# A ring of two halves of three groups, moved in 50688 bytes a partition, in place of six slots of one group

## The chip, the cores and the metric

The kernel runs on one core of a Trainium2 chip; the other cores have nothing to do with it. The metric is the device time of one execution in microseconds, less being better. Three engines of the core have work: VectorE (DVE) computes, SyncE (SP) issues every load, ScalarE (ACT) issues every store. The transfers themselves run on the core's 16 DMA engines.

## What is computed

The input has 8 batches of 4096 rows of 2112 float32 numbers. Every four rows that follow one another make a group; the mean of the group is taken from each of its rows.

```python
B, S, D = 8, 4096, 2112
stride = 4
x_r = x.reshape(B, S // stride, stride, D)
pooled = x_r.mean(axis=2)
upsampled = np.repeat(pooled, stride, axis=1)
return (x - upsampled).astype(np.float32)
```

So each number is read from HBM once and written once: 8 x 4096 x 2112 x 4 bytes = 276.8 MB in each direction. There is no reuse that could lessen it.

## The kernel before

Lines 27 to 37 look at the input as 8192 groups of 8448 numbers (four rows of 2112, which lie next to each other in HBM, 33792 bytes). One **tile** is 128 groups, one on each partition, 4224 KB in all; there are n = 64 tiles. A tile is a single run of 4.3 MB in HBM, and a load of it gives each partition a run of 33792 bytes.

Six slots in SBUF (line 46) hold one tile each; `pad` (line 45) only fills space ahead of them. Tile k goes through slot k mod 6, in place: loaded, changed by VectorE, stored from the same bytes. Two places for the sum take turns, `s_sb` in SBUF and `s_ps` in PSUM (lines 47 and 48).

The order of the work is written out by hand with semaphores inside `tile_critical` (line 78); no planner moves anything:

- **Loads** (lines 79 to 84) stand in the queue of SP, 64 in order. The load of tile k waits until the store of tile k-6 has landed, since both use one slot. The first six wait for nothing.
- **VectorE** (lines 86 to 90) runs `reduce_tile` for each tile, in a loop of 10 laps of six tiles, and four more behind it. Line 58 waits for the load. Line 59 adds rows 0 and 1 into the sum, line 62 adds rows 2 and 3 to it (two instructions of 2112 numbers a partition), and line 67 does x = sum * (-1/4) + x on all four rows at once, with the sum repeated by a stride of zero (one instruction of 8448 numbers). It then raises `done_sem`.
- **Stores** (lines 92 to 96) stand in the queue of ACT, 64 in order; the store of tile k waits for `done_sem` to reach k+1.
- SP waits at the end for the last six stores (lines 98 and 99).

Of the kernel before, what the change touches and what calls it, by code (L numbers as in the profile page):

```python
# [1 line left out]

# [4 lines left out]

STRIDE = 4
SLOTS = 6  # L10
PAD = 224


@with_exitstack
def kernel(
    ctx: ExitStack,
    tc: tile.TileContext,
    x: bass.AP,
    out: bass.AP,
):  # L20

    nc = tc.nc
    B, S, D = x.shape
    P = nc.NUM_PARTITIONS
    W = STRIDE * D  # L30
    G = (B * S) // STRIDE
    assert S % STRIDE == 0 and G % P == 0
    n = G // P

    xg = x.rearrange("b (g f) d -> (b g) (f d)", f=STRIDE)
    og = out.rearrange("b (g f) d -> (b g) (f d)", f=STRIDE)
    f32 = mybir.dt.float32

    pad_pool = ctx.enter_context(tc.tile_pool(name="pad", bufs=1))
    io_pool = ctx.enter_context(tc.tile_pool(name="io", bufs=1))  # L40
    sum_pool = ctx.enter_context(tc.tile_pool(name="sum", bufs=1))
    psum_pool = ctx.enter_context(
        tc.tile_pool(name="psum", bufs=1, space=bass.MemoryType.PSUM)
    )
    pad_pool.tile([P, PAD], f32, name="pad")
    slots = [io_pool.tile([P, W], f32, name=f"slot{b}") for b in range(SLOTS)]
    s_sb = sum_pool.tile([P, D], f32, name="s_sb")
    s_ps = psum_pool.tile([P, D], f32, name="s_ps")

    load_sems = [tc.alloc_semaphore(f"load{b}") for b in range(SLOTS)]  # L50
    store_sems = [tc.alloc_semaphore(f"store{b}") for b in range(SLOTS)]
    step_sem = tc.alloc_semaphore("step")
    done_sem = tc.alloc_semaphore("done")

    def reduce_tile(b, parity):
        rows = slots[b].rearrange("p (f d) -> p f d", f=STRIDE)
        s = s_ps if parity else s_sb
        nc.vector.wait_ge(load_sems[b], 16).then_inc(load_sems[b], -16)  # L58
        add = nc.vector.tensor_add(out=s[:], in0=rows[:, 0, :], in1=rows[:, 1, :])  # L59
        add.then_inc(step_sem)  # L60
        for f in range(2, STRIDE):
            add = nc.vector.tensor_add(out=s[:], in0=s[:], in1=rows[:, f, :])  # L62
            add._wait_ge(step_sem, f - 1)
            add.then_inc(step_sem)
        adds = STRIDE - 1
        nc.vector.wait_ge(step_sem, adds).then_inc(step_sem, -adds)  # L66
        nc.vector.scalar_tensor_tensor(  # L67
            out=rows,
            in0=s[:, None, :].to_broadcast([P, STRIDE, D]),
            scalar=-1.0 / STRIDE,  # L70
            in1=rows,
            op0=mybir.AluOpType.mult,
            op1=mybir.AluOpType.add,
        ).then_inc(done_sem)

    assert SLOTS % 2 == 0
    laps, rest = divmod(n, SLOTS)
    with tc.tile_critical():
        for k in range(n):
            b, lap = k % SLOTS, k // SLOTS  # L80
            load = nc.sync.dma_start(out=slots[b][:], in_=xg[k * P:(k + 1) * P])
            if lap:
                load._wait_ge(store_sems[b], 16 * lap)
            load.then_inc(load_sems[b], 16)

        with nc.vector.Fori(0, laps):
            for b in range(SLOTS):
                reduce_tile(b, b % 2)
        for b in range(rest):
            reduce_tile(b, b % 2)  # L90

        for k in range(n):
            b = k % SLOTS
            store = nc.scalar.dma_start(out=og[k * P:(k + 1) * P], in_=slots[b][:])
            store._wait_ge(done_sem, k + 1)
            store.then_inc(store_sems[b], 16)

        for k in range(n - SLOTS, n):
            nc.sync.wait_ge(store_sems[k % SLOTS], 16 * (k // SLOTS + 1))


# [1 line left out]
_INS = ['x']  # L103
_OUTS = [((8, 4096, 2112), 'float32')]


# [23 lines left out]
```

## Time and profile before

| What | Value |
|---|---|
| median of 10 executions | 1285.81 us (1285.6 to 1286.02) |
| the profiled execution, its own time | 1286.08 us |
| its span in the profile | 1284.3 us |
| moved by DMA | 553.66 MB, mean 431 GB/s |
| VectorE busy | 1026.5 us, 80% of the span |
| one load, issue to landing | least 12.6, median 59.7, most 91.2 us |
| one store, issue to landing | least 13.7, median 43.6, most 43.7 us |
| first load issued, first add | 0.95 us, 13.69 us |
| first store issued | 29.98 us |
| last load issued | 1192.89 us |
| last subtraction | starts at 1260.07 us, takes 8.96 us |

The span is the time between the first and the last thing in the profile of that one execution. The execution's own time is 1.8 us longer than the span, and 0.27 us over the median. In the profile a row of instructions gives the line, the engine, the operation, the tiles written and read, how many there were, their busy time in us and the mean of one in ns, and then the idle time of the engine ahead of them. In the views by stretches of time, the columns are the stretch, its length, the busy time of VectorE and GpSimd with the number of instructions, the granted clock of TensorE, the busy share of the 16 DMA engines, and the GB/s they moved.

### The profile page before, as it was taken

The page shows a single profiled execution, that of the slowest core. Times are in us where ns is not written, and L with a number is a line of the kernel's source. Part 1 is how long each engine was busy: PE and PEld are TensorE (multiplying, and loading weights), DVE is VectorE, ACT ScalarE, POOL GpSimd, SP SyncE. Part 2 cuts the span into 40 slices and gives each one's busy share as a digit, 9 for nine tenths or more (in the row PEclk, how much of TensorE's full clock was granted, in tenths as well). Part 3 has the DMA queues.
Part 4 walks back from the last instruction along what each step waited for, and adds up shares of the span by engine and source line. Part 5 has one row for each costly group of instructions (what it writes and reads, how often), then busy time and mean ns, then how long its engine had stood idle before and what let it go on. Part 6 is the DMA issues. An engine that isn't in the chain of part 4 may idle for free. (4 is left out here: it accounts for less than half of the span.)

```text
span 1284.3 us, 588 instructions
## 1 busy us (share of the span) xinstructions
DVE 1026.5 (80%) x256; POOL 0.2 (0%) x4
## 2 busy tenths in 40 slices
DVE  5998788787787877878778787787887878878775
POOL 0000000000000000000000000000000000000000
DMA  9999999999999999999999999999999999999999
GB/s 404 420 436 426 436 436 436 425 438 436 432 429 437 436 429 433 437 436 425 437 436 434 427 437 436 430 432 437 436 427 435 436 437 424 438 436 433 428 437 389
DMA packets 18433, 553.66 MB, mean 431 GB/s; under 512 B 2048, under 2 KB 2048, under 8 KB 2048
## 3 DMA queue, kind: packets, MB, share of 16 engines
q1 hardware_dynamic: 9216, 276.83, 50.0%
q10 hardware_dynamic: 9216, 276.83, 49.9%
q14 instruction: 1, 0.01, 0.0%
HBM read 276.82 MB, written 276.82 MB: 431 GB/s over the span
## 5 line engine op out<-in xcount | busy, mean ns | idle before, releaser
L67 DVE SCALAR_TENSOR_TENSOR slot<-s_sb,slot 128x8448 f32<-128x8448 f32 x32 | 286.7, 8958 | 4.7 <-DVEq L66 0.2
L67 DVE SCALAR_TENSOR_TENSOR slot<-s_ps,slot 128x8448 f32<-128x8448 f32 x32 | 286.6, 8957 | 4.7
L59 DVE TENSOR_TENSOR s_sb<-slot 128x2112 f32<-128x2112 f32 x32 | 75.4, 2357 | 120.7 <-DVEq L58 120.7
L59 DVE TENSOR_TENSOR s_ps<-slot 128x2112 f32<-128x2112 f32 x32 | 75.7, 2367 | 108.1 <-DVEq L58 108.1
L62 DVE TENSOR_TENSOR s_ps<-s_ps,slot 128x2112 f32<-128x2112 f32 x64 | 151.4, 2366 | 2.2
L62 DVE TENSOR_TENSOR s_sb<-s_sb,slot 128x2112 f32<-128x2112 f32 x64 | 150.9, 2358 | 2.2
L114 POOL MEMSET const-uint8-127<- 128x1 uint8 x1 | 0.1, 102 | 0.0
L114 POOL MEMSET const-bfloat16-1.0<- 128x1 bf16 x1 | 0.1, 101 | 0.0
L114 POOL MEMSET const-float32-0.0<- 128x1 f32 x1 | 0.1, 98 | 0.2 <-issue 0.2
L114 POOL MEMSET const-float32-1.0<- 128x1 f32 x1 | 0.1, 98 | 0.0
## 6 DMA issues: line engine op xcount, KB each, us to landing
slot<-in_x_dram SPq DMA_DIRECT2D x64, 4224.0 KB, 59.7
out_dram<-slot ACTq DMA_DIRECT2D x64, 4224.0 KB, 43.6
```

Source lines behind the costliest of these rows:

```text
L59: add = nc.vector.tensor_add(out=s[:], in0=rows[:, 0, :], in1=rows[:, 1, :])
L62: add = nc.vector.tensor_add(out=s[:], in0=s[:], in1=rows[:, f, :])
L67: nc.vector.scalar_tensor_tensor(out=rows, in0=s[:, None, :].to_broadcast([P, STRIDE, D]), scalar=-1.0 / STRIDE, in1=rows, op0=mybir.AluOp ...
L114: nc = _bacc.Bacc("TRN2", target_bir_lowering=False, num_devices=1)
```

## The change

The 64 tiles become 21 supers of three tiles each and one tile left over (21 x 3 + 1). A super is 384 groups; partition p now holds three groups that lie next to each other in HBM, 3p, 3p+1 and 3p+2 of the super (`adjacent`), a run of 101376 bytes. In place of six slots there is one ring of the same 6 x 33792 bytes a partition, in two halves of three groups.

A super is moved in two **parts** of one and a half groups, 50688 bytes a partition. So the first part holds the first group and the first two rows of the middle one, the second part the rest. In HBM the 128 runs of one transfer are 50688 bytes long and begin 101376 bytes apart; the other part fills the gaps. There are four parts in the ring, each with a semaphore for its load and one for its store. SP issues 42 loads of a part and one of the tile left over; ACT issues 42 stores of a part and two for the left over tile, of two rows each. The load of part i waits for the store of part i-4.

VectorE's loop runs 10 laps of two supers, and one super and the left over tile follow. In a super the first and last group are done as before. The middle group's first add is done ahead of the wait for the second part, the two others behind it, and its subtraction is two instructions of 4224 numbers a partition in place of one of 8448. The store of a super's first part waits for the first of these two (the second subtraction of the super), the store of its second part for the last subtraction of the super (the fourth).

```diff
-SLOTS = 6
+HALVES = 2
+SUPER = 3
+PARTS = 2
...
+    def adjacent(rows, k):
+
+        return rows.rearrange("(p j) w -> p (j w)", j=k)
...
-    slots = [io_pool.tile([P, W], f32, name=f"slot{b}") for b in range(SLOTS)]
+    ring = io_pool.tile([P, HALVES * SUPER * W], f32, name="ring")
...
+    n_parts = HALVES * PARTS
+    step = SUPER * W // PARTS
+    half_group = STRIDE // 2
...
+    for j in range(n_super):
+        src = adjacent(xg[j * SUPER * P:(j + 1) * SUPER * P], SUPER)
+        dst = adjacent(og[j * SUPER * P:(j + 1) * SUPER * P], SUPER)
+        for h in range(PARTS):
+            part = slice(h * step, (h + 1) * step)
+            a = (j % HALVES) * SUPER * W + h * step
+            moves.append((a, src[:, part], dst[:, part], subs * j + (2, subs)[h]))
...
+    def reduce_super(half, parity):
+        groups = [
+            Group((half * SUPER + j) * W, (parity + j) % 2) for j in range(SUPER)
+        ]
+        begin(half * PARTS)
+        groups[0].add(0, STRIDE)
+        groups[0].sub(0, STRIDE)
+        groups[1].add(0, half_group)
+        begin(half * PARTS + 1)
+        groups[1].add(half_group, STRIDE)
+        groups[1].sub(0, half_group)
+        groups[1].sub(half_group, STRIDE)
+        groups[2].add(0, STRIDE)
+        groups[2].sub(0, STRIDE)
+
+    def load(i, cols, src):
+        dma = nc.sync.dma_start(out=ring[:, cols], in_=src)
+        if i >= n_parts:
+            dma._wait_ge(store_sems[i % n_parts], 16 * (i // n_parts))
+        dma.then_inc(load_sems[i % n_parts], 16)
+
+    def store(i, cols, dst, done):
+        dma = nc.scalar.dma_start(out=dst, in_=ring[:, cols])
+        dma._wait_ge(done_sem, done)
+        dma.then_inc(store_sems[i % n_parts], 16)
...
+        with nc.vector.Fori(0, laps):
+            for half in range(HALVES):
+                reduce_super(half, half * SUPER % 2)
+        reduce_super(0, 0)
+        begin(len(moves) % n_parts)
+        last = Group(last_col, SUPER % 2)
+        last.add(0, STRIDE)
+        last.sub(0, half_group)
+        last.sub(half_group, STRIDE)
+
+        for i, (a, _, dst, done) in enumerate(moves):
+            store(i, slice(a, a + step), dst, done)
+        for h in range(2):
+            a = h * half_group * D
+            b = a + half_group * D
+            store(
+                len(moves),
+                slice(last_col + a, last_col + b),
+                og[last_rows, a:b],
+                subs * n_super + 1 + h,
+            )
```

`begin` is the wait for a part's load, `Group.add` the adds of a range of a group's rows and `Group.sub` the subtraction on a range of them, with the same instructions as before.

## The prediction, made before the changed kernel was run

> **What bounds the kernel now.** I read the page first. VectorE is busy 1026.5 of 1284.3 us, so it is not the bound. The row by slices and the queue rows say what is:
>
> ```profile
> DMA  9999999999999999999999999999999999999999
> ...
> q1 hardware_dynamic: 9216, 276.83, 50.0%
> q10 hardware_dynamic: 9216, 276.83, 49.9%
> ```
>
> The 16 DMA engines are busy in every slice, and the two queues together fill 99.9% of the span. Of 9216 packets in a queue, 8192 are runs of 33792 bytes (64 tiles x 128 partitions); the other 1024 are the ones under 512 B. Next the waits, to see whether VectorE or the transfers come last:
>
> ```profile
> DVE s_sb L59 <- DVEq L58: 120.7, 30, 13.7
> DVE s_ps L59 <- DVEq L58: 108.1, 30, 3.7
> ```
>
> VectorE waits some 3.7 us for the load of nearly each tile. The period is read from the timeline: the first add of tile 7 starts at 134.72, that of tile 63 at 1252.75, so (1252.75 - 134.72)/56 = 19.965 us a tile, in which 2 x 4224 KB (8.651 MB) pass: 433.3 GB/s. The view by stretches agrees, and shows loads alone (14 to 30), both (the next three) and stores alone (last):
>
> ```profile
> 14.00:30.00 16.00, 15.78 (x5) 0.00 (x0) 1.00 0.98 425
> 60.00:90.00 30.00, 29.57 (x9) 0.00 (x0) 1.00 1.01 436
> 90.00:120.00 30.00, 25.86 (x8) 0.00 (x0) 1.00 1.00 433
> 100.00:1100.00 1000.00, 803.96 (x201) 0.00 (x0) 1.00 1.00 433
> 1256.00:1280.00 24.00, 12.84 (x3) 0.00 (x0) 1.00 1.00 430
> ```
>
> The stretch 1281 to 1283 moves only 17 GB/s: the bytes end at about 1281. So the span is 2.3 us until the engines run, 64 x 19.965 = 1277.8 us of bytes, 3 us after the last byte, and about 1 us of ramp. Only three things can change the time: the rate, an interval without transfers, or the two ends. I take them in turn.
>
> **1. Intervals without transfers: 0.** This is where the ring could hurt, so I lay the new order out by hand with the old durations. A tile costs VectorE 16.17 us (13.69 to 29.86). A part is 6.488 MB: 15 us with the engines to itself, 30 us while loads and stores share them. Let the first part (A) of a super land at 0; the others then land at 30 (B), 60 and 90. First group: until 16.2. First add of the middle one: 18.6. Now the added wait: VectorE stands until B lands at 30, and queued behind that wait are the rest of this super and, through it, the store of A. Two adds (2 x 2.37) and half a subtraction (8.96/2) later, at 39.4, the store of A is issued; the other half ends at 43.9, the third group and with it the store of B at 60.0. VectorE is then done just as the next super's first part lands, so it keeps up: 48.7 us of work in 60. The subtraction cut in two adds at most one instruction's fixed part. By the rows 8958 ns for 8448 numbers is 1.060 ns each, so the 2358 ns add of 2112 holds about 118 ns beyond that: 0.12 us x 22 is 2.6 us, and the 228.8 us of waits above hide it. Uncovered, it would cost those 2.6 us.
>
> Does a part come back in time? A place is used every 4 x 30 = 119.8 us. For A: 30 loading, 39.4 held, 30 storing, so 20.4 us are left for standing in queues and for hand-overs (store landed, next load issued and running). For B: 30 + 30 + 30, so 29.8 left. One hand-over is at most 2.6 us by the first load (12.6 us to landing, 9.98 of them bytes). Two of them take 5.2 of the 20.4 us. So about 15 us of queue stand ready, less than now (119.8 - 16.2 - 2 x 20 = 63.6), but above zero. And as long as either queue holds a transfer, the engines are full: stores alone run at 430 above. Before the first store there is no hole either: it moves from 29.98 to about 45.5 us (A lands at 17.6, B at 32.6, then the steps above), but the four loads issued at the start hold the same 26 MB and last beyond 60 us. At the end the left over tile lands at 50 on the same clock; stores still queued then end at about 53, 68 (A), 83 (B), and 88 and 93 (the two halves), and VectorE has released these by 39, 60, 72 and 76. Each is ahead of its turn, so the engines run through to the last byte. What is late next after VectorE's waits is still the transfers.
>
> **2. The two ends: +0.3 us.** The first load is issued as early as now, the last byte is followed by the same 3 us. Only the stretch of loads alone grows, by 45.5 - 30 = 15.5 us. At 425 in place of 433 GB/s that costs 15.5 x 8/433 = 0.3 us; if the 425 is only the ramp, nothing.
>
> **3. The rate: between 0 and -2.6 us, -1.3 taken.** The runs grow from 33792 to 50688 bytes. There are 16384 of them now, and then 2 x 42 x 128 + 128 (the left over load) + 256 (its two stores) = 11136: 32% fewer. Transfers fall from 128 to 87. What a run costs beyond its bytes is not shown, as all have one size. From below: nothing, the rate belongs to the bytes; the 433 that stands in all long stretches speaks for that. From above: the best stretch of 30 us has 436; if the whole way from 433.3 to 436 (0.6% of 1277.8 = 7.9 us) were a fixed part of each run, 32% of it would go: -2.6 us. Both ends are as near to the rows (436 is one stretch whose edges blur by a packet or two), so I take the middle, -1.3. A loss of rate by the new pattern (runs 101376 bytes apart) has no row that shows it; it is bounded by 430 and 425, and priced as a rival.
>
> Here two rules of the Trainium skill can be set against the rows. "DMA: Bandwidth & Descriptors", section "Bandwidth", fits a transfer as 2.0 us and its bytes at 436 GB/s; 41 fewer transfers would then save 82 us. But by that fit the 128 transfers would take 1526 us in a row, and they take 1284.3: the fixed part lies under the next transfer here. The same page, "Where 436 GB/s comes from", sets a ceiling of 435.2 GB/s for the 16 engines; by it only 0.44%, 5.6 us by estimate, is left to win by any change of size, and 32% of that is 1.8 us. The same page's table of other facts tells of a rate halved where rows lie a large power of two apart, which speaks against spreading the runs; 101376 is not such a distance and no run here shows it.
>
> **Sum.** 0 + 0.3 - 1.3 = -1.0 us. The profiled execution took 1286.08 (span 1284.3 and 1.8 around it), so the changed one would take 1285.1 when profiled; that execution lies 0.27 over the median, so the median would be **1284.8 us**, -0.08%. A measurement of this kernel can tell about 0.2% (2.6 us) from no change.
>
> **The rivals.**
> - **Faster: the fixed parts are larger than I take them.** The share of 1.00 in the stretches is rounded, so up to 0.5% of 1277.8 us (6.4 us) could be gaps at the 128 hand-overs from transfer to transfer; 41 fewer save 2.0 us. With the full 2.6 us of the runs: -4.6, so 1281.2 us. For it: it takes only small fixed parts. Against it: the two queues overlap, so a gap in one is filled by the other. 0.15.
> - **Slower: the spread pattern lowers the rate.** Place: each load at line 131 and store at line 137. Today one transfer is one run of 4.3 MB; then it is 128 pieces, half of a 13 MB stretch. Price: at 430 GB/s (stores alone) 1277.8 x 3.3/430 = +9.8, so 1295.6; at 425, +25, so 1311. It decides from 432.4 GB/s down, which is +2.6. For it: rates of 425 to 436 show that direction or mixture may matter a little, and nothing in this trace was so spread. Against it: each piece is still 50 KB long. 0.14.
> - **Slower: the ring runs out.** If the 15 us of queue are used up (B's wait, hand-overs longer than 2.6 us), load and store queues are both empty once in each lap of 120 us. A hand-over each time, 2.6 us x 10, gives +26, so 1311 us. It decides once VectorE's hold and hand-overs together grow by those 15 us. 0.07.
> - **It does nothing measurable by itself.** Bytes set the time and the old fixed parts were hidden: 1285.8 to 1286.1. This lies in the bound of my forecast, as the forecast's small gain does.
>
> **How the numbers follow.** Forecast, 1283.2 to 1286.1, 0.62 (0.36 for a small gain, 0.26 for none); 0.02 for small losses within 0.2%; faster rival 0.15; slower rivals 0.14 and 0.07. That makes faster 0.15, same 0.64, slower 0.21. For 8 in 10 the range runs from the faster rival's 1281 to the 1295.6 of 430 GB/s; it leaves out the deeper half of the slower cases (0.11) and the gains above 4.8 us (0.05). The likeliest case's own range is 1283.2 to 1286.1.
>
> **What would show it.** Right: DMA still 9 in all 40 slices, 433 to 434 GB/s in the stretch 100 to 1100, first store issued near 45 us, VectorE waiting about 11 us at the wait for a second part and almost nothing at the one for a first part, loads landing after some 33 to 50 us rather than 59.7, and bytes ending 3 us ahead of the span's end. Step 1 is wrong if a slice falls under 9 or a long stretch under a DMA share of 0.99; step 3 if the share stays at 1.00 and the GB/s move away from 433 by over 1; step 2 if the first 60 us or the last 30 lose more than a microsecond against now.

## The result and the profile after

The changed kernel takes 1296.17 us (median of 8 executions, 1295.71 to 1297.12) against 1285.75 us: 1.0081 times as long, interval 1.0072 to 1.009. That is 10.4 us slower, where I had forecast 1.0 us less and a range that ended at 1295.6. The profiled execution took 1295.94 us (span 1294.2), 9.9 us over that of before. The median hides how far executions lie apart: of twelve on record, ten took 1295.7 to 1297.9 us, one 1289.6 and one 1285.8. Those of the kernel before stay within 0.5 us.

First the same two parts of the page as before, the slices and the queues:

```profile
DMA  9999999999999999999999999999999999999977
GB/s 401 426 442 436 426 434 442 426 428 447 429 426 443 434 426 440 437 426 436 439 428 432 437 432 426 440 431 431 439 429 434 439 429 429 439 434 426 435 340 339
...
q1 hardware_dynamic: 6192, 276.83, 49.6%
q10 hardware_dynamic: 6336, 276.83, 49.4%
```

There are a third fewer packets, as worked out. The engines are full through 38 slices, and the loss seems to be all in the last two (340 and 339 GB/s, where before had 437 and 389, as its own row shows):

```profile
GB/s 404 420 436 426 436 436 436 425 438 436 432 429 437 436 429 433 437 436 425 437 436 434 427 437 436 430 432 437 436 427 435 436 437 424 438 436 433 428 437 389
```

The view by stretches puts numbers to it (stretch, its length, busy time of VectorE and GpSimd, clock, DMA share, GB/s):

```profile
14.00:30.00 16.00, 10.87 (x4) 0.00 (x0) 1.00 1.00 434
100.00:1100.00 1000.00, 802.00 (x217) 0.00 (x0) 1.00 1.00 433
1250.00:1260.00 10.00, 9.82 (x3) 0.00 (x0) 1.00 0.59 256
1260.00:1270.00 10.00, 9.79 (x5) 0.00 (x0) 1.00 0.78 335
1280.00:1290.00 10.00, 0.00 (x0) 0.00 (x0) 1.00 0.77 329
```

From here one would say: the drain has an interval without transfers, since the store queue ran dry while VectorE still worked. The timeline of VectorE speaks against that as the whole story. These are the two adds that wait for the second part, early and late, and the last subtractions:

```profile
203.06 4.75 DVE L95 TENSOR_TENSOR s_sb<-s_sb,ring 128x2112 f32<-128x2112 f32 x2 [11.33 <-DVEq L83]
...
1231.87 4.77 DVE L95 TENSOR_TENSOR s_ps<-s_ps,ring 128x2112 f32<-128x2112 f32 x2 [11.27 <-DVEq L83]
...
1269.18 9.02 DVE L106 SCALAR_TENSOR_TENSOR ring<-s_ps,ring 128x4224 f32<-128x4224 f32 x2
```

The wait of 11 us for the second part is the one I had laid out. But (1231.87 - 203.06)/17 = 60.52 us a super, where 3 x 19.965 = 59.90 us went before, from these two rows, 56 tiles apart:

```profile
134.72 2.37 DVE L59 TENSOR_TENSOR s_ps<-slot 128x2112 f32<-128x2112 f32 x1 [3.73 <-DVEq L58]
...
1252.75 2.37 DVE L59 TENSOR_TENSOR s_ps<-slot 128x2112 f32<-128x2112 f32 x1 [3.74 <-DVEq L58]
```

The loads land later and later, by 0.6 us a super, though the sum of all engines still reads 433 GB/s.

What the sum hides is in the trace's records of single DMA packets (start, duration, bytes, queue). They don't name the engine; I followed each engine from a packet's end to the next packet's start, which gives 16 chains, without gaps until the end. Two chains that meet in phase can be taken for each other from there on, and in this trace two do, at 917 us. Durations of a run of 33792 bytes are 1251 ns before, nearly without exception; a run of 50688 takes 1872 ns. "Slow" is a packet of over 50 ns more, between 100 and 1230 us:

```
                slow loads  slow stores  excess, all  ends of the 16 engines: first, middle, last
before                   0            0       0.0 us  1281.4  1281.5  1282.3
after                   84            3      20.1 us  1287.9  1287.9  1292.5
```

After, load packets are at times 0.05 to 1.35 us late, and most of it falls on one chain: 6.86 us up to 917 us and 5.67 us behind it, 12.5 us in all. It is one engine on both sides of 917 us: its packets never pause and it ends at 1292.5, while each of the other 15 pauses for 6.7 to 8.4 us near the end. Its packets between 110 and 1200 us take 60.50 us a super, the period of the landings; without the lateness they would take 59.81. The kernel's semaphores ask for all 16 engines, so VectorE, the stores and the next loads go at the pace of the slowest. The pauses of the other 15, which end at 1242 and 1262 us, are what the stretches show. The sum is -1.8 us (rate, below) + 12.5 us = 10.7, and the last byte came 10.2 us later than before.

### The profile page after: what moved, and what is told of

Read it like the earlier page. It is cut to its first block, busy times and chain, and to the rows that moved or that the text cites. A ratio compares the mean times of both kernels' runs of the same rounds, so it can differ in the third digit from the quotient of the medians.

```text
span 1294.2 us, 547 instructions
## 1 busy us (share of the span) xinstructions
DVE 1023.7 (79%) x278; POOL 0.2 (0%) x4
## 5 line engine op out<-in xcount | busy, mean ns | idle before, releaser
L106 DVE SCALAR_TENSOR_TENSOR ring<-s_ps,ring 128x4224 f32<-128x4224 f32 (+1 forms) x44 | 287.4, 6554 | 4.7
L106 DVE SCALAR_TENSOR_TENSOR ring<-s_sb,ring 128x8448 f32<-128x8448 f32 (+1 forms) x42 | 287.3, 6861 | 4.7 <-DVEq L103 0.2
L95 DVE TENSOR_TENSOR s_ps<-s_ps,ring 128x2112 f32<-128x2112 f32 x64 | 151.4, 2366 | 115.8 <-DVEq L83 114.0
L95 DVE TENSOR_TENSOR s_sb<-s_sb,ring 128x2112 f32<-128x2112 f32 x64 | 150.9, 2358 | 106.6 <-DVEq L83 104.7
L95 DVE TENSOR_TENSOR s_sb<-ring 128x2112 f32<-128x2112 f32 x32 | 75.2, 2350 | 21.0 <-DVEq L83 21.0
L95 DVE TENSOR_TENSOR s_ps<-ring 128x2112 f32<-128x2112 f32 x32 | 75.5, 2360 | 1.7 <-DVEq L83 1.7
```

The lines of the kernel that those rows point to most:

```text
L95: add = nc.vector.tensor_add(out=self.s[:], in0=first, in1=self.rows[:, f, :])
L106: nc.vector.scalar_tensor_tensor(out=self.rows[:, lo:hi, :], in0=self.s[:, None, :].to_broadcast([P, hi - lo, D]), scalar=-1.0 / STRIDE, i ...
```

## The experiments

Times are medians beside the kernel before on the same chip, which ran at 1285.69 to 1285.78 us. e1 to e4 ran on one chip, e5 to e8 on a second, e9 to e14 on a third. P, Q and L are the three theories named at e1: the spread rows, the small lead of the loads, the long runs.

**e1, the changed kernel again.** No edit.

> The changed kernel once more, unaltered, to see whether its profile is steady. Three theories stand: (P) the runs that begin 101376 bytes apart make some load packets of one DMA engine slow, and that engine ends last; (Q) the ring keeps too little in the queue of loads, so that packets at the head of a transfer show their latency; (L) runs of 50688 bytes are themselves prone to it. All three: 1294 to 1298 us, one DMA engine with 10 us and more of slow packets, and the rate of the engines falling below 400 GB/s in the last 50 us.

1292.86 us, 1290.08 to 1296.53 in five executions (ratio 1.0053, 1.0035 to 1.0072). In its profile are 89 slow loads and 4 slow stores, 26.5 us in all, and the last engine ends 4.6 us behind the middle one. The picture is steady, the amount is not.

**e2, each transfer one whole run in HBM.**

```diff
-        src = adjacent(xg[j * SUPER * P:(j + 1) * SUPER * P], SUPER)
+        src = adjacent(xh[j * SUPER * 2 * P:(j + 1) * SUPER * 2 * P], SUPER)
...
-            moves.append((a, src[:, part], dst[:, part], subs * j + (2, subs)[h]))
+            block = slice(h * P, (h + 1) * P)
+            moves.append((a, src[block], dst[block], subs * j + (2, subs)[h]))
```

(`xh` views the input as rows of half a group; `dst` likewise.)

> The changed kernel with every transfer one whole run of 6.49 MB in HBM: the parts of a super are two blocks one behind the other, partition p holding the p-th run of 50688 bytes. Ring, sizes, waits and VectorE's instructions stay; since groups then straddle partitions, VectorE subtracts means of other rows than the reference's, at the same cost. P: no slow packets, about 1284 us (the steady rate of the changed kernel is 433.6 in place of 433.3 GB/s, and the queues run dry only late). Q and L: 1294 to 1298 us.

1289.15 us, with executions from 1284.65 to 1296.86, half of them over 1290 (ratio 1.0033, 1.0007 to 1.0059). 41 slow loads in its profile, and again one engine 4.8 us behind. P had asked for none: the spread in HBM is not needed for them.

**e3, the kernel before with runs spread in HBM.**

```diff
-            load = nc.sync.dma_start(out=slots[b][:], in_=xg[k * P:(k + 1) * P])
+            load = nc.sync.dma_start(out=slots[b][:], in_=place(xg, k))
```

(`place` gives group r of the super j, with j, r = divmod(k, 3), from partition rows of three groups; the store likewise.)

> The kernel before with its six slots, waits and runs of 33792 bytes; only the place in HBM changes: a slot takes one of three neighbouring groups, so that the runs of a transfer begin 101376 bytes apart. P: slow packets here too, 1290 us or more. Q and L: 1285.8 us as before.

1285.67 us, ratio 1.000 (0.999 to 1.001), no slow load. With e2 this ends P, the rival I had given 0.14.

**e4, the kernel before with four slots.** The edit is `SLOTS = 4`.

> The kernel before with four slots in place of six: runs of 33792 bytes, each transfer one whole run of 4.3 MB, but 24 us in place of 64 us of a slot's turn are left for queues and hand-overs (80 - 16.2 - 20 - 20), about as in the changed ring (20.4). Q: slow packets and an emptier end, 1289 us or more. P and L: 1285.8 to 1287 us.

1290.39 us (ratio 1.0038, 1.0023 to 1.0052), in Q's range, but not by Q's mechanism: one slow load in the profile, all engines ending within 0.2 us. About 0.8 us is lost at the start, the rest at the end. The first line is the last tile's first add, the others are stretches:

```profile
1259.65 2.37 DVE L59 TENSOR_TENSOR s_ps<-slot 128x2112 f32<-128x2112 f32 x1 [3.75 <-DVEq L58]
```

```profile
1260.00:1270.00 10.00, 9.79 (x4) 0.00 (x0) 1.00 1.00 433
1270.00:1280.00 10.00, 5.92 (x1) 0.00 (x0) 1.00 0.55 237
```

The last load lands 6.9 us later than before (1252.75), the stores have meanwhile caught up, and all 16 engines stand for 4.5 us until VectorE is done. So here a shallower ring cost mainly a pause at the end.

**e5, all transfers of the changed kernel cut in two.**

```diff
-        dma = nc.sync.dma_start(out=ring[:, cols], in_=src)
...
+        mid = (cols.stop - cols.start) // 2
+        for lo, hi in ((0, mid), (mid, 2 * mid)):
+            dma = nc.sync.dma_start(
+                out=ring[:, cols.start + lo:cols.start + hi], in_=src[:, lo:hi]
+            )
...
```

(The stores likewise; each of the two raises the semaphore by 16, and the waits ask for 32.)

> The changed kernel with each transfer cut in two of half the columns, both behind the same wait: ring, order, waits and VectorE stay, and a run has 25344 bytes in place of 50688 (twice as many runs). Where long runs are what makes load packets slow (L): no slow packets, all DMA engines end within 2 us of each other, 1284 to 1288 us. Where it is the small lead of the load queue (Q): one engine still ends 4 us and more behind, 1290 to 1297 us.

1288.11 us, 1287.79 to 1288.77 (ratio 1.0018, 1.0009 to 1.0028): two slow loads, engines together. Same ring, same waits, and the executions no longer scatter.

**e6, the first super by whole groups.** Three loads and three stores of 33792 bytes with their own semaphores, and VectorE's loop then takes the halves in the order 1, 0:

```diff
+        for g, (cols, src, _) in enumerate(groups0):
+            nc.sync.dma_start(out=ring[:, cols], in_=src).then_inc(first_loads[g], 16)
...
+        for g, (cols, _, dst) in enumerate(groups0):
+            dma = nc.scalar.dma_start(out=dst, in_=ring[:, cols])
+            dma._wait_ge(done_sem, g + 1)
+            dma.then_inc(first_stores[g], 16)
```

> The changed kernel with its first super moved and computed by whole groups (three loads and stores of 33792 bytes a partition, with semaphores of their own), so that the first store goes out near 30 in place of 47 us; all else stays, runs of 50688 bytes too. Q: the lead of the load queue grows by some 8 us for the whole run, slow packets go, 1283.5 to 1286 us. L: slow packets stay, 1289 to 1297 us.

1287.07 us; nine executions at 1286.55 to 1287.36 and one at 1300.65 (ratio 1.0021, 0.9999 to 1.0043). No slow load in the profile. The lead of a load, from the landing of the store that it waits for to its own first packet, is 12.7 us through the whole run; it is 39.1 us before, and 8.5 falling to 3.8 us in the changed kernel. This spoke for Q, though one execution in ten, at 1300.65 us, is slower than any of the changed kernel. The start itself lost about 2 us more than before (by the bytes that its packets had moved at 100 us), so the time is not the hoped-for 1285.

**e7, the kernel before with a late first store.**

```diff
-            store._wait_ge(done_sem, k + 1)
+            store._wait_ge(done_sem, 3 if k == 0 else k + 1)
```

> The kernel before (six slots, runs of 33792 bytes) with one wait changed: the first store waits for the third tile, so it goes out near 62 in place of 30 us, when the loads of the start have run out. The share of a slot's turn left for queues stays 64 us, but it moves from the queue of loads to that of stores. Q: slow packets through the run, several us above what the start itself loses (an interval of about 4 us without transfers, so 1290 us). L: no slow packets, 1289 to 1290.5 us.

1287.07 us (ratio 1.0011, 1.0002 to 1.0021), lead 8.5 us, no slow load at all. Both theories had asked for 1289 us or more, so the interval at the start cost less than I expected. A small lead alone, with runs of 33792 bytes, brings no slow packets: Q alone falls.

**e8, the last super's stores cut in four.**

```diff
+            if i >= len(moves) - PARTS:
+                first = W if i % PARTS == 0 else step - W
+                for lo, hi, d in ((0, first, done - 1), (first, step, done)):
+                    store(i, slice(a + lo, a + hi), dst[:, lo:hi], d)
+            else:
+                store(i, slice(a, a + step), dst, done)
```

> The changed kernel with the stores of the last super cut in four (by groups and half groups, each behind its own subtraction): only the drain at the end changes. If the interval without transfers at the end is what costs (D): 1285 to 1287 us. If the DMA engine with the slow packets sets the end (L and Q): 1290 to 1296 us, as before this edit, and that engine shows no interval without transfers.

1296.44 us (ratio 1.0076, 1.006 to 1.0092): eight executions at 1295.85 to 1297.43, two near 1287. The pause at the end, which is what the page shows first, is not the cause: the edit meant to fill it gains nothing, and in the trace of the changed kernel the engine that ends last has no pause. The profile here is one of the two quick executions, with 37 slow loads spread over several engines, the last of which ended at 1283.8. Its stretches show no pause; of a slow execution with this edit there is no trace.

```profile
1250.00:1260.00 10.00, 9.93 (x4) 0.00 (x0) 1.00 1.04 444
1260.00:1270.00 10.00, 9.85 (x3) 0.00 (x0) 1.00 0.97 421
```

**e9, whole transfers of halved runs.**

```diff
-            moves.append((a, src[:, part], dst[:, part], subs * j + (2, subs)[h]))
+            moves.append((a, pairs(x, i), pairs(out, i), subs * j + (2, subs)[h]))
```

(`pairs` gives each partition two runs of 25344 bytes from two whole blocks; the ring's side is seen as `p (q w) -> p q w`.)

> The ring, order, waits and transfers of 6.49 MB of the changed kernel, but each partition's 50688 bytes of a transfer are two runs of 25344 from two blocks in HBM that are each whole (numbers move in HBM, so the means are of other rows than the reference's; VectorE's work is the same). So the size of a transfer stays and its runs are halved, where the run with halved transfers had halved both. If the length of a run matters: no slow packets, all DMA engines end together, near the 1288.1 us of that run. If the size of a transfer matters: slow packets on one engine, 1290 us and more.

1287.12 us, 1286.77 to 1287.75 (ratio 1.0011, 1.0001 to 1.002). 30 slow loads, where I had asked for none, but they are spread and small: 5.5 us in all, 0.7 us on the worst engine. So late loads occur with short runs too, but here without a loss of several microseconds. That loss goes by the length of the run, not by the size of the transfer.

**e10 and e11, only loads or only stores halved.** The edit of e5 in `load` alone, and in `store` alone.

> The changed kernel with the loads alone cut in two of half the columns (runs of 25344 bytes), the stores with runs of 50688. If long loads become slow of themselves: no slow packets, 1286 to 1288 us. If they are slow because a long store packet is in their way: slow packets stay, 1290 us or more.

> The reverse: stores in runs of 25344 bytes, loads in runs of 50688. If long loads become slow of themselves: slow packets stay, 1290 us or more. If a long store packet is in their way: none, 1286 to 1288 us.

With long stores and short loads 1331.59 us (ratio 1.0368, 1.0351 to 1.0385): 584 slow loads and 484 slow stores, 379.7 us together, 23.7 us for each of the 16 engines on average. With short stores and long loads 1287.11 us (1.0012, 1.0003 to 1.0022): seven slow loads, 1 us in all. The long stretch and part of the end of e10:

```profile
100.00:1100.00 1000.00, 773.44 (x211) 0.00 (x0) 1.00 1.00 424
1260.00:1270.00 10.00, 2.12 (x1) 0.00 (x0) 1.00 0.57 243
1270.00:1280.00 10.00, 9.82 (x4) 0.00 (x0) 1.00 0.25 106
```

So the long runs that matter are those of the stores: of L, half holds. The chains show one thing more: an engine takes packets of the two queues in turn, one each, so of unequal runs the longer queue moves more bytes and then stands empty. One engine of e11, and one of the kernel before and after, L a load packet and S a store packet. The packets of 4 bytes that raise a semaphore take a turn too and are left out here; where two letters of one kind meet in the row of after, such a packet stood between them.

```
before  L S L S L S L S L S L S L S L S L S L S L S L S L S L S
after   L S L S L S L L S L S S L S L S L S L S L S L L S L S S
e11     L S L S L S L S L S S S S S S S S S S L S L S L L S L S
```

In e11 the queue of loads is empty for ten store packets in each turn, with leads of 4 us, and its loads are still not slow. In e10 that unevenness adds to the loss (the queue of stores stands empty for some 26 load packets in a turn, and at the end most engines pause for about 14 us up to 1278 us and 5.5 us up to 1298 us), so its 46 us are not the price of long stores alone.

**e12, e6 and e8 together.** Both edits.

> The changed kernel with both ends fine: first super moved by groups (which had made the slow packets go, at 1287.07 us), and the last super's stores cut in four. No slow packets; the 0.8 us without transfers at 1255 to 1260 us goes: 1286.0 to 1286.6 us, about the kernel before. Lower than 1285.2 would mean that the fewer runs pay more than I see.

1287.11 us, one execution of ten at 1301.14 (ratio 1.0022, 1.0 to 1.0045): not below e6, so the 0.8 us at the end were not worth that. I had expected no slow packets and 1286.0 to 1286.6 us; its profile has 17 slow loads, 3.3 us in all, though the lead stays near 13 us.

**e13, e6 with its first stores late; e14, the middle group without its wait.** For e13:

```diff
-            dma._wait_ge(done_sem, g + 1)
+            dma._wait_ge(done_sem, SUPER)
```

For e14:

```diff
-        groups[1].add(0, half_group)
+        groups[1].pair(0)
+        groups[1].sub(0, half_group)
         begin(half * PARTS + 1)
-        groups[1].add(half_group, STRIDE)
-        groups[1].sub(0, half_group)
+        groups[1].s = s_sb
+        groups[1].pair(half_group)
         groups[1].sub(half_group, STRIDE)
```

(`pair` puts the sum of two neighbouring rows into `s`.)

> The kernel whose first super is moved by groups (run e6, steady at 1287.07 us, each load ready 12.7 us ahead of its turn and no slow packets) with one wait changed: its first three stores wait for all three groups, so the first goes out near 62 in place of 30 us and the loads of the start run out first. Long runs, ring and VectorE's work stay. If the small lead of the loads is the condition (Q): the lead falls to some 8 us or less, slow packets come back in most executions, 1290 us and more. If it was the finer start by itself that helped: no slow packets, 1288 to 1291 us by the interval at the start alone.

> The changed kernel with the middle group's wait taken apart: its two halves are treated as two groups of two rows (means of two rows, eight adds a super in place of nine), so that the first part needs nothing of the second and is released some 16 us sooner. If VectorE's wait for the second part is the cause: no slow packets, 1284 to 1286 us. If the small lead of the loads is (Q), which the start sets and not VectorE's hold: slow packets stay in most executions, 1290 us and more.

e13: 1290.28 us, 1287.97 to 1291.59 (ratio 1.0038, 1.0024 to 1.0052). Its slow loads are back (8.0 us in all between 100 and 1230 us), but the lead had not fallen as I expected: it is 12.6 us and erodes to 10.3. e14: 1287.05 us, from 1284.5 to 1296.41, half of ten over 1288 (1.0022, 1.0002 to 1.0042). Its profile is the quickest execution, with a lead of 5.4 us, smaller than in the changed kernel, and two slow loads. So neither the lead nor VectorE's wait decides it alone, and Q as a second condition is not shown.

All runs but e10 together, by the run length of the stores, with every execution on record. Another choice of the packets' edges moves a lead by some half a microsecond.

```
kernel                 store run   lead, us       executions, us
before                     33792   39.1           1285.6 to 1286.4
e3 spread                  33792   39.4           1285.6 to 1286.0
e7 late first store        33792   8.5 to 7.9     1286.7 to 1288.1
e4 four slots              33792   8.4            1290.0 to 1291.3
e5 halves                  25344   7.9            1287.8 to 1288.8
e9 pairs                   25344   8.4            1286.8 to 1287.8
e11 store halves           25344   4              1286.5 to 1287.5, one 1290.5
after, e1                  50688   8.5 to 3.8     1285.8 to 1297.9
e2 dense                   50688   8.4 to 3.8     1284.7 to 1296.9
e14 uncoupled              50688   5.4            1284.5 to 1296.4
e13 late start             50688   12.6 to 10.3   1288.0 to 1291.6
e8 end                     50688   7.6 to 7.0     1286.9 to 1297.4
e6, e12                    50688   12.7, 13       1286.6 to 1287.8, two of 20 over 1300
```

But for one execution of e11, scatter of several microseconds goes with stores of 50688 bytes and only with them. The chip does not explain it: on each of the three, a version with such stores scattered (e1 and e2; e8; e14) beside steady ones with shorter stores (e3; e5 and e7; e9). No version beat the kernel before beyond the noise; the quickest executions, of e2 (1284.65) and e14 (1284.5), are the lowest on record.

## Why the prediction was wrong

- **Step 1, intervals without transfers: 0. Failed here.** The layout was right in what it laid out: first store at 46.98 us (45.5), 11 us of waiting for a second part, nearly none for a first. What failed is that it treated the 16 engines as one. It asked only whether some queue holds a transfer, and had no term for an engine that falls behind the others. One did, by 12.5 us, and with semaphores that count 16 engines, it set the landings of all. The sign that I had named for step 1 appeared, a slice under 9 (the last two read 7). The drain, where I had let each store be "ahead of its turn", then had pauses on the other 15 (share 0.59 and 0.78); e8 shows that an edit to fill them doesn't help.
- **Step 1, the 15 us of queue.** I pooled them. In the run nearly all of it stood in the store queue: the store that a load waits for landed only 8.5 us ahead of that load's first packet. Of this the hand-over is 4.8 us by the first one, where the queue was empty; I had reckoned 2.6. e4 prices a shallow ring by itself: +4.7 us, nearly all at the end. The rival "the ring runs out" had this place, but not this course; the spread pattern had the direction and nearly the size (1295.6), but by luck: e3 refutes it.
- **Step 2, +0.3 us: 0.** Loads alone ran at 434 GB/s between 14 and 30 us in the changed kernel. The 425 of before was no slower rate: the view books a packet where it starts, and with each packet counted by its time inside the stretch, before moves 433 there too. The sign for step 2, a loss in the last 30 us, appeared all the same, through the engine that came late.
- **Step 3, -1.3 us of 0 to -2.6: right, with -1.8.** The undisturbed rate is read from e6, whose adds behind the wait for a second part come at

```profile
150.27 4.77 DVE L105 TENSOR_TENSOR s_ps<-s_ps,ring 128x2112 f32<-128x2112 f32 x2 [11.38 <-DVEq L93]
...
1226.81 4.77 DVE L105 TENSOR_TENSOR s_ps<-s_ps,ring 128x2112 f32<-128x2112 f32 x2 [11.28 <-DVEq L93]
```

  so (1226.81 - 150.27)/18 = 59.81 us a super, 0.087 us less than before: -1.8 us over 21 supers. e9, with runs of 25344, has (1224.02 - 204.74)/17 = 59.96:

```profile
204.74 4.75 DVE L101 TENSOR_TENSOR s_sb<-s_sb,ring 128x2112 f32<-128x2112 f32 x2 [11.42 <-DVEq L89]
...
1224.02 4.77 DVE L101 TENSOR_TENSOR s_ps<-s_ps,ring 128x2112 f32<-128x2112 f32 x2 [11.42 <-DVEq L89]
```

- **The fit set against the rows.** The 2.0 us and 436 GB/s stand in the Trainium skill, "DMA: Bandwidth & Descriptors", in the section "Anatomy of one DMA" for transfers issued from GpSimd, and not in "Bandwidth". This kernel issues none from there, and the sum does not use the fit.
- **The chances.** 0.21 stood for slower, and the range ended 0.6 us short. The rate of 100 to 1100 us, my own test for step 3, stayed at 433, so by it step 3 held; the landing times would have been the test for what did happen.

**What stays open.** Shown: slow load packets, mostly on one engine, account for the loss of the profiled execution. A loss of this size went with long stores (e5, e9, e11 against the changed kernel and e10); long loads, spread rows and the pause at the end do not bring it. Single late loads occur with short stores too (e9). Not shown: why a long store makes a load packet late, why one engine more than others, and what, beside long stores, decides how often an execution falls into it. In e6 and e12, with a finer start and a lead near 13 us, it was 2 of 20, but e13, e14 and the 17 slow loads of e12 don't fit the lead as the cause.

## What to carry to other kernels

Where one sum of GB/s says that the DMA engines are full, ask also whether all 16 end together: compare the period of the landings (here 60.52 us) with the period that the bytes give (59.81), since the slowest engine sets the first. Where a transfer is already at its ceiling, count what fewer and longer runs can still gain (here 1.8 us of 1286) before paying for it with the depth of the ring. And look at single executions, not only at the median: a kernel that scatters over 10 us has something that its profile, being one of them, may not show.

## What the runs showed of the hardware

- A run costs about 5 ns beyond its bytes, by estimate. Per engine a super has 64, 48 or 32 runs of 25344, 33792 or 50688 bytes and takes 59.96, 59.90 or 59.81 us: 3.9 and 5.4 ns for each run less. Without that part, at 4.9 ns, it would be 59.66 us, 435.0 GB/s, an estimate. The Trainium skill, "DMA: Bandwidth & Descriptors", section "Where 436 GB/s comes from", gives 435.2 as the ceiling; the estimate from the runs comes close to it.
- While both queues hold work, their packets alternate one for one on an engine, at runs of 25344, 33792 and 50688 bytes (the sequences above).
- Rows 101376 bytes apart cost nothing measurable against whole runs of 4.3 MB (e3: ratio 1.000, 0.999 to 1.001).
- Beside stores of 50688 bytes, load packets came late by up to 1.35 us (the changed kernel, mostly on one engine) and in bulk (e10, 584 of them). With stores of 25344 they were few or small (e11, seven; e9, 30 of 5.5 us in all).
